# Interleaving three mixers, and letting the scheduler pick ScalarE or VectorE, in a two-layer hybrid decoder trunk

## The chip, the cores and the metric

The kernel runs on all 8 cores of one Trainium2 chip, two dies of four cores. Every core does the same program on its own prompt sequence of 2048 positions and 16 sample tokens; no core talks to another. The metric is the device time of the slowest core in microseconds (us). Most runs of one kernel agree within 0.3%. Some executions fall into a slower state, whatever the kernel: one die shows a lower granted clock and is over 1% longer.

The views of the profile use short names: PE is TensorE (PEld its weight loads), DVE is VectorE, ACT is ScalarE, POOL is GpSimd, SP is SyncE; L12 is line 12 of that run's kernel.py. PSUM is the memory that takes PE's results; this kernel uses it as eight banks.

## The reference, cut to what matters

```python
D_MODEL = 1024; SEQ = 2048; DEPTH = 2; C_A = C_B = 384; C_C = 256; K_A = 31; K_B = 3; CHUNK = 128; D_FF = 2816

def mixer(h, buf_a, buf_b, w_in, ...):
    z = h @ w_in                                             # ONE input projection, 2432 columns
    a_val, a_gate, b_x, b_b, b_c, c_u, c_v = jnp.split(z, SPLITS, axis=-1)
    hist_a = jnp.concatenate([buf_a, a_val * jax.nn.sigmoid(a_gate)], axis=1)             # A
    ya = jax.nn.silu(layernorm(causal_dwconv(hist_a, dw_a) + dw_a_bias, ln_a_g, ln_a_b))
    hist_b = jnp.concatenate([buf_b, b_c * b_x], axis=1)                                  # B
    yb = b_b * causal_dwconv(hist_b, conv_b_w)
    u = jax.nn.gelu(c_u)                                                                  # C
    vn = layernorm(jax.nn.gelu(c_v), ln_c_g, ln_c_b)
    yc = u * chunk_spatial(vn, w_s, b_s)
    return jnp.concatenate([ya, yb, yc], axis=-1) @ w_o, ...

for i in range(DEPTH):
    x = x + mixer(rmsnorm(x, norm_mix_g[i]), ...)
    gate, up = jnp.split(rmsnorm(x, norm_ffn_g[i]) @ w_ffn_in[i], 2, axis=-1)
    x = x + (jax.nn.silu(gate) * up) @ w_ffn_out[i]
return rmsnorm(x, norm_final_g)
```

## The kernel before

The kernel is written as a list of operations with their buffers. A list scheduler inside it (the "placer") then simulates the engines with rough costs and fixes, once and for all, the order in which each engine will execute. The order in the source sets an operation's priority (`due`); the placer departs from it when something later is ready earlier. ScalarE pays for a change of its function table, so an operation of another table set is put off by 3000 ns of priority. A matmul ahead of the program's order (`nd is not base`) gets a PSUM bank only while three of the eight are free.

```python
pick = None
for nd in cand[e]:
    if self._ready(nd, base, free) <= s + 30.0:
        d = nd.due
        if e == "act" and nd.table and nd.table != table:
            d += 3000.0
        if pick is None or d < pick[0]:
            pick = (d, nd)
# ... (cut)
def _ready(self, nd, base, free):
    # ... (cut)
    if new:
        if len(free) < new or (nd is not base and len(free) < 3):
            return 1e12
        r = max(r, min(free)[0])
```

The start: five column blocks (of 256, 272 and three times 512 columns, in this order) are loaded, normalised and projected for mixer A. Squares, Ln and Exp of the norms and the sigmoid of the gate are all ScalarE's.

```python
def sq_one(b, m):                        # 8 of these make one block's sum of squares
    act(AF.Square, sqt[si][:, 0:n], xT[:, m, c0:c0 + n], [b_x[m][b]], [b_sqt[si]])
    mm(pi[:, 0:n], [(ones_b[:], sqt[si][:, 0:n])], [b_sqt[si], b_const], pi, i == 0, i == 7)
# ... (cut)
def unit_a(b, j):
    pg = proj(("in", l, j), 0, b)                            # gate, one PSUM bank
    act(AF.Sigmoid, E[:, 0:n], pg[:, 0:n], [pg], [bE])       # another table set than Ln and Exp
    pv = proj(("in", l, j), 1, b)
    tt(phased(hist_a[:, j, :])[:, h0:h0 + nh], by(pv), by(E), ALU.mult, [pv, bE], [B[("ha", b)]])
```

The mixer's order, and the last step of mixer A. The convolution borrows the space of three of the eight residual rows (`xT[:, 5:8]`); `x_back` fetches them again.

```python
for q in range(2):
    for b in order:
        unit_cu(q, b)                    # all of u
# ... (cut)
for cp in range(8):
    unit_cv(cp)                          # v, its LayerNorm and the spatial product
    if cp >= 1:
        unit_conv(conv.popleft())        # mixer A's convolution, 12 of these
# ... (cut)
for j in range(3):
    for b in order:
        unit_b(j, b)                     # mixer B, three slices
        if conv:
            unit_conv(conv.popleft())
# ... (cut)
def ln_silu(g2):                         # mixer A's result, out to memory and back as yaC
    # ... (cut)
    k.dma("sp", yscr[l, j]..., poly[:, 8 * j:8 * j + 8, 4:4 + NN], ...)
    k.dma("sp", yaC[:, j, :], yscr[l, j], reads=[B[("yscr", j)]], writes=[B[("ya", j)]])

def x_back():
    # ... (cut)
    k.dma("sp", xT[:, 5:8, c0:c0 + n], src[:, :, c0:c0 + n], writes=[b_x[m][b] for m in range(5, 8)])
```

## Time and profile before

| before | |
|---|---|
| time, median of the first 4 runs | 1483.86 us (1482.32 to 1485.8) |
| PE, DVE, ACT busy | 95%, 40%, 26% |
| start and first mixer, until the first feed-forward flows | 286.6 us |
| first feed-forward, unbroken on PE | 466.8 us |
| second mixer | 237.0 us |
| second feed-forward, unbroken on PE | 466.2 us |
| end: last norm and output | 25.3 us |

The stages come from the chain of waits, which has one unbroken PE piece for each feed-forward; the 25.3 is a median over the cores. These are the two pieces in the kernel before (columns: start in us, length in us, what; x counts instructions), on its slowest core. The gap between the end of the first and the start of the second, 990.41 - 286.60 - 466.77, is the second mixer.

```profile
286.60 466.77 PE ps L482 x2683
...
990.41 466.21 PE ps L482 x2681
```

### The profile page before, as it was taken

The numbers are of one execution on the slowest core, as the hardware profiler recorded it, in microseconds if no ns is written. First come the engines' busy times: TensorE is split into PE (matmuls) and PEld (weight loads), VectorE is DVE, ScalarE is ACT, GpSimd is POOL, SyncE is SP. The second block draws the span as 40 slices with busy tenths as digits, with TensorE's granted clock in tenths as the row PEclk, the third lists the DMA queues.
The fourth block names the chain that finished last, engine by engine and source line by source line (L and its number), as shares of the span: only waits on it lengthen the run. The fifth ranks groups of instructions, "written<-read, shape, count | busy, mean of one in ns | idle before, by whom it ended". The sixth has DMA issues, their size and how long they took to land.

```text
span 1481.9 us, 23505 instructions; the slowest of 8 cores (1477.1 to 1481.9 us)
## 1 busy us (share of the span) xinstructions
PE 1405.1 (95%) x8288; PEld 798.4 (54%) x8288; DVE 594.3 (40%) x1179; ACT 385.9 (26%) x748; POOL 78.4 (5%) x156
## 2 busy tenths in 40 slices
PE   2797999999999999999999999999999999999995
PEld 1346654655555555555555755465555555555553
DVE  1536678632222222222282587863222222222237
ACT  3423633431110011111262452343111001111124
POOL 0002100000000000000000210000000000000000
PEclk9998999999999999999999999999999999999998
DMA  9744571124122221222243558021412312121106
GB/s 229 168 100 82 102 192 25 31 42 72 22 48 40 43 38 35 35 36 53 50 105 92 105 102 200 16 33 26 72 21 48 53 29 39 34 45 20 30 1 230
DMA packets 51490, 101.56 MB, mean 69 GB/s; under 512 B 5104, under 2 KB 25104, under 8 KB 51344
## 3 DMA queue, kind: packets, MB, share of 16 engines
q0 software_dynamic: 16704, 56.63, 22.9%
q1 hardware_dynamic: 34672, 43.43, 10.0%
q8 instruction: 70, 1.15, 0.3%
q14 instruction: 44, 0.36, 0.1%
HBM read 138.51 MB, written 19.63 MB: 107 GB/s over the span
## 4 chain that ended last, share of the span: by engine, by line
PE 88%; DVE 6%; issue 3%; DMA 1%; ACT 1%; POOL 0%; SPq 0%; DVEq 0%; ACTq 0%; POOLq 0%
PE ps L482 88%; DMA xT<-x_in 1%; DVE shr L470 1%; DVE hT L470 1%; ACT shr L460 1%; DVE bnst L818 1%; DVE xT L470 1%; DVE vtok L478 0%; DVE hT L467 0%; DVE xT L467 0%; ACT shr L464 0%; POOL rs L824 0%; DVE bnmv L820 0%; SPq L204 0%; DVE tC L470 0%
## 5 line engine op out<-in xcount | busy, mean ns | idle before, releaser
L482 PE MATMUL ps<-hT,ring 128*128 128x512 bf16 (+3 forms) x5168 | 924.3, 338 | 11.0 <-DVE hT L467 6.5
L482 PEld LDWEIGHTS ps<-hT,ring 128*128 128x128 bf16 x5168 | 505.4, 98 | 408.0 <-issue 18.6
L467 DVE TENSOR_TENSOR gT<-ps,fs 128x512 bf16<-128x512 f32 (+2 forms) x220 | 129.4, 588 | 478.4 <-PE ps L482 478.4
L482 PE MATMUL ps<-gT,ring 128*128 128x512 bf16 (+2 forms) x1760 | 311.8, 338 | 0.0
L460 ACT ACTIVATE fs<-ps 128x512 f32<-128x512 f32 (+2 forms) x220 | 113.1, 514 | 639.4 <-PE ps L482 603.9
L482 PEld LDWEIGHTS ps<-gT,ring 128*128 128x128 bf16 x1760 | 171.9, 98 | 135.3
L467 DVE TENSOR_TENSOR xT<-ps,xT 128x512 f32<-128x512 f32 (+2 forms) x240 | 139.3, 586 | 221.3 <-PE ps L482 221.1
L460 ACT ACTIVATE shr<-xT 128x512 bf16<-128x512 f32 (+2 forms) x224 | 114.6, 548 | 215.3 <-DVE xT L467 119.1
L470 DVE SCALAR_TENSOR_TENSOR hT<-xT,pD,shr 128x512 bf16<-128x512 f32 (+2 forms) x160 | 95.2, 642 | 40.9 <-ACT shr L460 40.9
L482 PE MATMUL ps<-shr,ones_b 128*128 128x512 bf16 (+2 forms) x200 | 53.7, 352 | 39.7 <-ACT shr L460 38.4
L467 DVE TENSOR_TENSOR hist<-ps,ev 128x512 bf16<-128x512 f32 (+1 forms) x60 | 34.8, 582 | 75.7 <-PE ps L482 61.1
L482 PE MATMUL ps<-yaC,ring 128*128 128x512 bf16 (+1 forms) x240 | 56.1, 339 | 0.0
L204 POOL DMA_DIRECT2D ring<-w_fi x44 | 23.2, 528 | 604.3 <-PE ps L482 604.3
L482 PEld LDWEIGHTS ps<-shr,ones_b 128*128 128x128 bf16 x200 | 19.6, 99 | 63.6 <-issue 50.8
L460 ACT ACT_TABLE_LOAD x27 | 34.6, 1283 | 28.5 <-PE ps L482 15.8
L482 PE MATMUL ps<-u_t,ring 128*128 128x512 bf16 (+2 forms) x160 | 41.4, 341 | 0.0
L470 DVE SCALAR_TENSOR_TENSOR shr<-hist,pAB,shr 128x512 f32<-128x512 bf16 (+1 forms) x60 | 36.8, 640 | 2.6 <-DVE shr L470 0.5
L204 POOL DMA_DIRECT2D ring<-w_fo x32 | 16.9, 530 | 318.2 <-PE ps L482 302.2
L482 PEld LDWEIGHTS ps<-yaC,ring 128*128 128x128 bf16 x240 | 23.6, 98 | 18.7 <-issue 0.8
L482 PE MATMUL ps<-poly,ring 128*128 128x256 bf16 x240 | 31.7, 288 | 1.8 <-ACT gv L460 1.2
L482 PE MATMUL ps<-ring,hT 128*128 128x256 bf16 (+1 forms) x272 | 31.0, 273 | 0.3 <-ACT gv L460 0.3
L467 DVE TENSOR_TENSOR xT<-xT,lnA 128x512 f32<-128x512 f32 x48 | 30.1, 684 | 0.1
(79 smaller groups left out, 434.7 us busy)
## 6 DMA issues: line engine op xcount, KB each, us to landing
ring<-w_fi POOLq DMA_DIRECT2D x44, 512.0 KB, 5.2
ring<-w_fo POOLq DMA_DIRECT2D x32, 352.0 KB, 4.3
ring<-w_in POOLq DMA_DIRECT2D x18, 512.0 KB, 7.3
ring<-w_tp POOLq DMA_DIRECT2D x12, 640.0 KB, 9.7
xT<-x_in SPq DMA_DIRECT2D x6, 1024.0 KB, 19.3
y_out<-xT SPq DMA_DIRECT2D x6, 1024.0 KB, 5.0
ring<-w_o POOLq DMA_DIRECT2D x8, 512.0 KB, 5.2
hscr<-hist SPq DMA_DIRECT2D x6, 512.0 KB, 11.1
```

The lines of the kernel that those rows point to most:

```text
L204: fn = lambda eng: eng.dma_start(out=out, in_=in_)
L460: k.op("act", lambda e: e.activation(out=ap(out), in_=ap(in_), func=func, bias=bias, scale=scale), reads, writes, width(out), SETS.get(func))
L467: k.op("dve", lambda e: e.tensor_tensor(out=ap(out), in0=ap(a), in1=ap(b), op=op), reads, writes, width(out))
L470: k.op("dve", lambda e: e.scalar_tensor_tensor(out=ap(out), in0=ap(in0), scalar=scalar, in1=ap(in1), op0=op0, op1=op1), reads, writes, wid ...
L482: k.node("pe", [((lambda e, p=p: e.matmul(ap(p[0]), lhsT=p[1], rhs=p[2], start=p[3], stop=p[4])), max(width(p[0]), 40) * 0.43, p[5] if len ...
L818: k.op("dve", lambda e, t=t: e.bn_stats(out=bn[0:np_, t, :], in_=G(t)), [bG], [B[("bn", z)]])
```

## The change

Its intent is to fill PE's bubbles in the mixers: interleave work that loads VectorE with projections that load PE, let elementwise work go to whichever of ScalarE and VectorE would finish it first, send mixer A's result ahead of the residual, and let PE run further ahead in PSUM. The diff, cut to its core:

```diff
+        def either(self, choices, reads, writes, n):        # a node with alternatives
...
-                if len(free) < new or (nd is not base and len(free) < 3):
+                if len(free) < new:
+                    return 1e12
+                if nd is not base and sum(1 for b in self.live if b.T > base.T) >= self.BANKS_AHEAD:   # 4
                     return 1e12
...
-            act(AF.Square, sqt[si][:, 0:n], xT[:, m, c0:c0 + n], [b_x[m][b]], [b_sqt[si]])
+            square(sqt[si][:, 0:n], xT[:, m, c0:c0 + n], [b_x[m][b]], [b_sqt[si]])   # ACT or DVE
...     (bias add and copies of the convolution, copy and first tap of mixer B: the same way)
-                    k.dma("sp", xT[:, 5:8, c0:c0 + n], src[:, :, c0:c0 + n], writes=[...])
+                    k.dma("sp", xT[:, 5:8, c0:c0 + n], src[:, :, c0:c0 + n],
+                          [B[("yscr", j)] for j in range(3)] + [B[("ya", j)] for j in range(3)], [...])
...     (weights: a dictionary, fetched in the order of first use, in place of a fixed list)
-            for q in range(2):
-                for b in order:
-                    unit_cu(q, b)
...     (the loops over unit_cv and unit_b of before)
+            for b in order:
+                unit_cu(0, b)
+                unit_cu(1, b)
+                for cp in range(8):
+                    if blk(2 * cp) == b:
+                        unit_cv(cp)
+                unit_b(0, b)
...
+                convs((0, 1, 1, 2, 2)[order.index(b)])
...
+            convs(6)
+            for j in (1, 2):
                 for b in order:
                     unit_b(j, b)
+                    convs(2 if j == 1 and b != order[4] else 0)
```

Because weights are now fetched on demand and mixer B's first slice ("in", 0, 5) has no entry in the list of held loads, it is fetched at the very start, in the middle of the input.

The whole diff also holds back the set-up of mixer C's mask until the last block is normalised.

## The prediction

> **What bounds the kernel now.** I read the cores first, to know whether a die was disturbed. It is not: the dies differ by 0.8 us in 1480, at one clock.
>
> ```profile
> die 0 (median of its cores): 1479.8 us, clock 0.989
> die 1 (median of its cores): 1479.0 us, clock 0.988
> ```
>
> Then the page: busy shares, the slices, and the chain that ended last.
>
> ```profile
> PE 1405.1 (95%) x8288; PEld 798.4 (54%) x8288; DVE 594.3 (40%) x1179; ACT 385.9 (26%) x748; POOL 78.4 (5%) x156
> ...
> PE   2797999999999999999999999999999999999995
> ...
> DVE  1536678632222222222282587863222222222237
> ...
> PE 88%; DVE 6%; issue 3%; DMA 1%; ACT 1%; POOL 0%; SPq 0%; DVEq 0%; ACTq 0%; POOLq 0%
> ```
>
> PE carries 88% of the chain. The two flat stretches of 9s are the feed-forward blocks, which no part of the change can shorten. What can move is where the PE row falls under 9 or the DVE row climbs to 6 to 8: the start, the two mixers, the end. PE 95% busy overstates its use, since ends of matmuls are modelled, so I counted columns. In full flow, in the last feed-forward, 11 matmuls of 512 columns take 2.54 us of which the last is 0.38, so one costs (2.54-0.38)/10 = 0.216 us, 0.422 ns a column. Times the columns of the matmuls listed in each stretch this gives useful PE time; the rest is lost time. Stretch by stretch (PE, PEld, DVE, ACT, POOL busy, then PE clock, DMA share, GB/s):
>
> ```profile
> 0.00:70.00 70.00, 34.12 (x149) 16.73 (x150) 24.39 (x48) 30.35 (x58) 3.49 (x10) 0.98 0.86 210
> 70.00:120.00 50.00, 50.00 (x306) 29.01 (x304) 15.58 (x37) 13.76 (x25) 1.78 (x4) 1.00 0.49 114
> 120.00:170.00 50.00, 39.20 (x346) 29.17 (x344) 38.37 (x109) 22.22 (x45) 12.20 (x24) 0.90 0.44 72
> ...
> 220.00:240.00 20.00, 16.53 (x96) 8.82 (x94) 19.59 (x46) 3.12 (x7) 0.53 (x1) 1.00 0.32 90
> ...
> 1440.00:1482.00 42.00, 26.31 (x156) 15.01 (x154) 28.57 (x52) 20.95 (x42) 0.00 (x0) 0.85 0.59 203
> ```
>
> Lost by columns: 46 us in 0 to 70; 13 in 120 to 170 (the chunk mixer C and the convolution of layer 0), 9.5 in the same phase of layer 1 (830 to 880); 3.5 in 220 to 240 and 5 in 920 to 950 (the gated mixer B), plus 1.5 each just before the two feed-forwards; 17 in the last 32 us. Together about 97 us. In 120 to 170 DVE is busy 38 of 50 us, yet in the 50 us before it only 16, while PE was full: the work is badly placed in time. In 220 to 240 DVE is saturated (19.6 of 20) and ACT nearly idle (3.1).
>
> What VectorE does there, and the DMA queue just before:
>
> ```profile
> L467 DVE TENSOR_TENSOR xT<-ps,pPP 128x512 f32<-128x512 f32 x24 | 15.7, 684 | 4.2 <-PE ps L482 3.9 <-issue 0.3
> L474 DVE TENSOR_SCALAR shr<-hist,pAB 128x512 f32<-128x512 bf16 x18 | 8.7, 481 | 0.6 <-ACT hist L464 0.6
> L460 ACT ACTIVATE shr<-xT 128x512 bf16<-128x512 f32 x144 | 84.4, 622 | 177.2 <-DVE xT L467 99.8 <-PE ps L482 75.2 <-DVE hT L470 2.0
> ```
>
> ```profile
> 198.76 0.80 SPq L204 DMA_DIRECT2D yscr<-poly  x1
> 199.65 8.47 SPq L204 DMA_DIRECT2D xT<-x_in  x5
> 208.28 6.57 SPq L204 DMA_DIRECT2D yaC<-yscr  x3
> ```
>
> The second fence matters: the return of the residual (five transfers, 3.1 MB) is queued ahead of the mixer A result that the output projection needs (yaC), so that result starts 9 us late.
>
> **What the Trainium skill says.** "VectorE: DVE Perf Modes", The TRN2 errata: an fp32 tensor_tensor takes (N+151)/0.96 ns, 691 for 512; the trace has 684 to 692. "ScalarE: Activation LUTs", What ACT_TABLE_LOAD costs: 186 ns + 0.833 a column, about 93 more per pointer operand, back-to-back ones overlapping by about 93. That is 613 for a square of 512 (trace 622), and 585 for 256 columns with two pointers (trace: 596). The same section has the table load at 1283 ns; the trace has 27 at a mean of 1283. "TensorE: Matmul & The Clock Gate", What's actually happening: PE drops to half rate after about 3.4 us idle. The trace agrees: after a wait of 4.46 us the clock of 130 to 140 is 0.56, so a bubble costs more than its own length. "DMA: Bandwidth & Descriptors", Queues, rings and completion order: each DMA engine takes turns among its queues; so an extra weight load shares bandwidth with the input.
>
> **The change part by part.**
> 1. *Order in the mixer.* Before: all of u, then eight v units with convolutions, then B. After: per block u, v, the first B slice and some convolutions. Matmuls are unchanged. A v unit costs DVE 2x(424+182+413+476+410) = 3.8 us, eight of them 30.5 us, packed against 14 us of projection. Spread over u, v, B0 and six convolutions (14+14+14+9 = 51 us of PE, with 30.5+3.4+4 = 38 us of DVE), PE becomes the slower one. I expect the lost 13 and 9.5 us to fall to 4 and 3.5: gain 15.
> 2. *Work that may go to either engine.* The 12 bias adds of a layer (684 ns of DVE each) can go to ACT as two activations, estimated from the skill's formula 2x493-93 = 0.9 us; squares and copies (ACT about 0.61) can go to DVE at 0.69; the 15 first taps of mixer B in a layer go to ACT, about 0.6 each. In the B phase DVE spends per 512-block 3x(481+748+748+684) = 8 us, 32 a layer, against 20.6 us of PE projection. Without the 481s it is 26, and ACT has room.
> 3. *yaC before the residual.* It no longer waits behind 8.5 us of queueing. Output projections of finished blocks can fill PE holes while DVE does B. The price: the last three row blocks of the residual arrive later, after five projections of the first block (5x1.7 us) at best. Parts 2 and 3 together: 3.5+5+1.5 of loss to about 4, gain 6.
> 4. *PSUM rule.* A matmul ahead of program order could take a bank only if three of eight were free; now up to four ahead-banks may be live, down to none free. It lets PE run ahead, and can also let ahead work sit on banks. No own gain credited.
> 5. *Weights on demand.* The slice of B0 now has a fresh ring place and no hold, so it is fetched right behind the first slice, in the input phase. On the software queue 3.28 MB took 29.6% of 70 us on all engines; so 0.52 MB costs an estimated 3.3 us, and block arrivals slip by about that.
> 6. *Start.* Blocks go round a loop of Ln and Exp 1.3, eight scalings on DVE 5.4 and a PE wait of 3 us, about 10 us each. Sharing squares with DVE, idle 5 us between blocks, may save 2 us on two blocks: 4 us. Four matmul groups of B0 can fill idle PE, but their second halves wait for the history buffer to be written out and keep banks. With part 5: gain 1, very unsure.
> 7. *End.* DVE is busy 28.6 of 42 us with residual adds and final scalings, which stay on DVE. Gain 0 to 1; taken as 0. Delaying the setup of masks: DVE work of 1.5 us moved only; 0.
>
> Sum: 15 + 6 + 1 = 22 us; 1484 - 22 = 1462; I shade it to **1460 us**, because bubbles that vanish also keep the PE clock up.
>
> **The rivals.**
> A. *The wait moves rather than vanishes.* Three weight slices (12 of the ring's 26 KB a partition) now stay live together through the interleaved phase. Taps for convolutions 4 and 5 can load only after the last u, later ones after the last v and B0, each taking 9.7 us to land. For: ring arithmetic. Against: B1's weights do not hang on those, so PE has 14 us of other work. If it bites in both layers: 5 to 8 us back, 1467 to 1470.
> B. *The start gets worse.* The extra load delays the second block, whose arrival (26.4 us) is on the chain, and held banks starve PE. For: DMA share 0.86 in 0 to 70, and that chain. Against: from 33 us the loop, not arrival, sets the pace. Time: 1465 to 1472.
> C. *Much more is won at the start:* more PE backlog done before 66 us, because ACT, freed from squares, serves the waiting sigmoids sooner. For: 46 us lost there, the largest pool. Against: table switches, and DVE has 5.4 of scaling plus 2 of gating per block. Time: 1440 to 1450.
> D. *Mixer losses are PE-only bubbles of latency, not DVE load:* then balancing gives little, 1475. DVE at 38 of 50 busy, and the idle 16 before, speak against it.
>
> **Range and chances.** A or B in part, or C in part, move the centre by 10 either way; two of them together by 15 to 18. Range 1442 to 1475. Two per cent below 1483.9 is 1454.2, 6 us under the centre, which needs C or a near-total recovery: 0.34. Within 2%: 0.63. Slower by over 2% would need a PSUM block of 30 us: 0.03.
>
> **What would show it.** Step 1: in the phase after the sigmoids DVE busy is spread at 7 to 8 tenths over some 60 us, with no PE wait on the v scalings (6.8 us before) and no clock under 0.9; ACT has bias activations. Steps 2 and 3: yaC is issued ahead of the residual, and the B phase has no PE wait on DVE over 1 us. Step 5: the third weight load within 5 us of the start, the last input block landing near 51 us. Feed-forward unchanged at 466 us of unbroken chain. I am wrong if the mixer stretches lose as much as before, or if the gain comes from the first 70 us.

## The result, and the profile after

The changed kernel takes 1450.2 us, the median of 8 runs (1448.9 to 1451.59). All runs of the kernel before have the median 1484.67. The ratio is 0.9769, with a 95% interval of 0.9759 to 0.9779. A ratio here is always the mean time of one kernel's fast runs over that of the other's of the same rounds, so not quite the ratio of the medians. Executions in which one die ran at a lower clock are left out of the means. The kernel is faster by 2.3%, some 34 us, where 24 were predicted.

The changed kernel's page, in the order of the lines that the prediction shows:

```profile
PE 1397.7 (96%) x8288; PEld 796.2 (55%) x8288; DVE 611.7 (42%) x1206; ACT 385.0 (27%) x731; POOL 78.8 (5%) x156
...
PE   3999999999999999999999999999999999999995
...
DVE  2657997522223222223573488762222332222237
...
PE 88%; DVE 4%; issue 2%; SPq 2%; DMA 2%; ACT 1%; DVEq 0%; POOL 0%; ACTq 0%; POOLq 0%
```

The second digit of the PE row went from 7 to 9: that is the start, from about 37 to 74 us. The fourth went from 7 to 9: that is the first mixer. VectorE as a whole is busy for 17 us more (611.7 against 594.3), so the gain is not relief of VectorE. It is work done at other moments. On the chain, SyncE's queue and the transfers have a larger share (0 to 2% and 1 to 2%), VectorE a smaller one (6 to 4%).

The same stretches as before, on the slowest core (us; PE, PEld, DVE, ACT, POOL busy; PE clock, DMA share, GB/s):

```profile
0.00:70.00 70.00, 42.16 (x229) 23.39 (x230) 30.11 (x66) 28.22 (x48) 3.50 (x10) 0.98 0.85 208
70.00:120.00 50.00, 50.00 (x325) 29.54 (x322) 29.28 (x70) 21.14 (x34) 6.96 (x14) 1.00 0.52 116
120.00:170.00 50.00, 47.96 (x369) 31.50 (x364) 41.36 (x100) 26.16 (x56) 8.29 (x17) 0.97 0.60 97
...
220.00:240.00 20.00, 20.00 (x94) 9.09 (x93) 14.24 (x23) 7.95 (x12) 0.00 (x0) 1.00 0.00 1
```

In 120 to 170 PE is busy for 48 us rather than 39, at a clock of 0.97 rather than 0.90. VectorE's work has moved into the 50 us before, 29 us where there were 16. And in the first 70 us PE issued 229 matmuls instead of 149.

The chain of waits of the kernel after (start, length, what):

```profile
34.04 18.29 DMA xT<-x_in
52.87 10.47 DMA ring<-w_in
63.48 1.91 PE ps L520 x12
...
66.87 72.22 PE ps L520 x478
...
262.51 466.41 PE ps L520 x2682
...
957.32 466.21 PE ps L520 x2681
```

At the start the chain of this core now goes through input and weight transfers until 63 us and then, but for two squares of 1.29 us, through PE for 72 us unbroken. On cores 0, 2, 3, 5 and 6 it goes through the third block's norm and scalings until 47 to 50 us and then through PE and the same two squares. The norms of the last two blocks, which it followed in the kernel before, are otherwise off it there. The stages on the slowest cores: start and first mixer 286.60 to 262.51, 24.1 us less; second mixer 237.04 to 228.40, 8.6 less; the rest, by difference, 0.5, of which 0.36 is in the first feed-forward.

To split the first of these I counted useful PE time as in the prediction (columns of the matmuls times 0.422 ns). On the slowest core of each kernel:

| done by | 70 us | 100 us | 140 us | 180 us |
|---|---|---|---|---|
| before | 22.4 | 52.3 | 81.1 | 117.6 |
| after | 34.3 | 64.3 | 103.7 | 138.5 |
| difference | 11.9 | 12.0 | 22.6 | 20.9 |

So by 70 us the changed kernel is 11.9 us of PE work ahead (8.6 on core 3, where before had 25.9). The slowest core of before was also the one with least done by 70 us; by the medians of all eight cores the lead is 9.5 us (25.2 and 34.7). Between 100 and 180 us it gains another 8.9 (10.3 by the medians), and the last 3.2 of the 24.1 come after 180 us, in mixer B and the output projection.

What happened at the start is a matter of ScalarE's order. ScalarE in the kernel before (start, length, then engine, line, operation, out<-in, count and, in brackets, idle time and its releaser): the last norm's Exp, the switch of the table, the first of the waiting sigmoids.

```profile
60.14 0.63 ACT L460 ACTIVATE shr<-shr 128x512 f32<-128x512 f32 x1
61.89 1.28 ACT L460 ACT_TABLE_LOAD   x1 [1.12 <-PE ps L482]
63.18 0.38 ACT L460 ACTIVATE ev<-ps 128x256 f32<-128x256 f32 x1
```

PE of the same kernel just then: it stops after 24 matmuls, and what lets it go on is that sigmoid.

```profile
59.04 3.64 PE L482 MATMUL ps<-hT,ring 128*128 128x512 bf16 x24
63.71 1.09 PE L482 MATMUL ps<-hT,ring 128*128 128x272 bf16 x8 [1.03 <-ACT ev L460]
```

ScalarE in the kernel after: the same table switch comes after the third norm, not the fifth, 18 us earlier.

```profile
41.42 0.63 ACT L486 ACTIVATE shr<-shr 128x512 f32<-128x512 f32 x1
...
44.15 1.28 ACT L486 ACT_TABLE_LOAD   x1
45.45 0.38 ACT L486 ACTIVATE ev<-ps 128x256 f32<-128x256 f32 x1
```

PE in the kernel after, while the fifth block was still coming in (until 52.3 us) and the fourth and fifth had their norms still ahead of them:

```profile
48.02 11.52 PE L520 MATMUL ps<-hT,ring 128*128 128x256 bf16 x64 [1.02 <-DVE hist L505]
```

In these twelve microseconds PE of before had small pieces, four matmuls of a norm or one of a projection, with waits for ScalarE and VectorE between them. That the order of ScalarE *causes* the gain is a theory at this point. The experiments test it.

The smaller signs that the prediction asked for. The elementwise work did spread: seven of the 24 bias adds went to ScalarE (14 activations of 256 columns, 472 ns each), and 16 of the 18 first taps of 512 columns. The groups view of the kernel after (line, engine, operation, shapes, count | busy us, mean ns | idle before and its releaser):

```profile
L789 ACT ACTIVATE xT<-ps,pPP 128x256 f32<-128x256 f32 x14 | 5.8, 472 | 4.0 <-PE ps L520 4.0
L954 ACT ACTIVATE shr<-hist,pAB 128x512 f32<-128x512 bf16 x16 | 10.5, 712 | 18.8 <-DVE hT L505 18.6
```

PE's waits on the v scalings fell from 6.8 us to 1.9 (the waits of PE in the kernel after: us in total, times, longest):

```profile
PE ps L520 <- DVE vtok L516: 1.9, 1, 1.9
```

And SyncE's queue sends yaC before the residual:

```profile
186.00 3.62 SPq L215 DMA_DIRECT2D yaC<-yscr  x3
197.49 4.07 SPq L215 DMA_DIRECT2D xT<-x_in  x5
```

### The profile page after: what moved, and what is told of

The parts are those of the page before. It is cut to its first block, busy times and chain, and to the rows that moved or that the text cites. A ratio compares the mean times of both kernels' runs of the same rounds, so it can differ in the third digit from the quotient of the medians.

```text
span 1448.7 us, 23408 instructions; the slowest of 8 cores (1445.8 to 1448.7 us)
## 1 busy us (share of the span) xinstructions
PE 1397.7 (96%) x8288; PEld 796.2 (55%) x8288; DVE 611.7 (42%) x1206; ACT 385.0 (27%) x731; POOL 78.8 (5%) x156
## 4 chain that ended last, share of the span: by engine, by line
PE 88%; DVE 4%; issue 2%; SPq 2%; DMA 2%; ACT 1%; DVEq 0%; POOL 0%; ACTq 0%; POOLq 0%
PE ps L520 88%; SPq L215 2%; DMA xT<-x_in 1%; DVE shr L508 1%; DMA ring<-w_in 1%; DVE xT L501 1%; DVE xT L508 1%; DVE hT L505 0%; ACT shr L493 0%; ACT shr L486 0%; DVE hist L505 0%; DVE xT L505 0%; DVE hT L508 0%; DVE shr L494 0%; ACT shr L497 0%
## 5 line engine op out<-in xcount | busy, mean ns | idle before, releaser
L493 ACT ACTIVATE shr<-xT 128x512 bf16<-128x512 f32 (+2 forms) x175 | 92.3, 547 | 208.9 <-DVE xT L505 101.9
L505 DVE TENSOR_TENSOR hist<-ps,ev 128x512 bf16<-128x512 f32 (+1 forms) x60 | 34.8, 582 | 45.5 <-PE ps L520 35.3
L494 DVE TENSOR_TENSOR shr<-xT 128x512 bf16<-128x512 f32 (+2 forms) x49 | 29.0, 611 | 20.9 <-DMA xT<-x_in 17.1
L520 PE MATMUL ps<-ring,hT 128*128 128x256 bf16 (+1 forms) x272 | 31.5, 273 | 0.5 <-DMA ring<-w_in 0.5
L501 DVE TENSOR_TENSOR xT<-xT,lnA 128x512 f32<-128x512 f32 x48 | 30.2, 684 | 0.0
```

The costliest lines, as they stand in the source:

```text
L493: k.either({"act": lambda e: e.activation(out=out, in_=a, func=AF.Square), "dve": lambda e: e.tensor_tensor(out=out, in0=a, in1=a, op=ALU. ...
L494: "dve": lambda e: e.tensor_tensor(out=out, in0=a, in1=a, op=ALU.mult)}, reads, writes, width(out))
L501: f = lambda e: e.tensor_tensor(out=out, in0=a, in1=b, op=op)
L505: k.op("dve", lambda e: e.tensor_tensor(out=ap(out), in0=ap(a), in1=ap(b), op=op), reads, writes, width(out))
L520: k.node("pe", [((lambda e, p=p: e.matmul(ap(p[0]), lhsT=p[1], rhs=p[2], start=p[3], stop=p[4])), max(width(p[0]), 40) * 0.43, p[5] if len ...
```

## The experiments

Twelve kernels ran, each beside runs of the kernel before on its own chip. All gave correct results. For each I give two stages besides the time: *first* is the time to the first feed-forward, *second* the second mixer, each a median over the cores whose chain shows it. *First* is counted back from the end of the first feed-forward by the 466.4 us that it takes in the kernel after, since in some runs (s1, x4) its unbroken piece begins 2 us late. The kernel before has 284.3 and 237.0, the one after 261.0 and 228.3; feed-forwards and end never moved by more than 0.6 us. Two theories of the start stood against each other. S: the earlier sigmoids make the gain. Q: the freedom of the squares, which shortens each norm, makes it. The expectations name a third, P: the new PSUM rule makes it; m4 and x4 bear on that. For the mixers, the question was which part of the change made which gain, and whether the parts add up or act only together (I, interaction).

### s1: before, with the sigmoids of two blocks ahead of the fourth norm

```diff
-            act(AF.Square, sqt[si][:, 0:n], xT[:, m, c0:c0 + n], [b_x[m][b]], [b_sqt[si]])
+            act(AF.Square, sqt[si][:, 0:n], xT[:, m, c0:c0 + n], [b_x[m][b]] + list(after), [b_sqt[si]])
...
-                        sq_one(b, m)
+                        sq_one(b, m, [B[("ha", order[0])], B[("ha", order[1])]] if i == 3 and m >= 4 else ())
```

> The kernel before, with one dependency added: the last four squares of the fourth input block wait until the gating of the first two blocks is done, so ScalarE takes the waiting sigmoids before the last two norms. Theory S (the start is gained because the sigmoids are served before the last two norms, which lets TensorE work off the first blocks while the rest of the input arrives): about 10 us faster than before, 1472 to 1477. Theory Q (the start is gained because squares are shared with VectorE) and theory P (because of the new PSUM rule): no gain, 1482 to 1488, or slower by the two extra table loads.

Measured 1475.22 us (1474.71 to 1476.96), ratio 0.9941 [0.9925, 0.9956]. First 271.1, 13.2 less than before; second 242.3, 5.3 more. ScalarE's timeline shows the switch at 50.6 us instead of 61.9:

```profile
50.57 1.28 ACT L460 ACT_TABLE_LOAD   x1 [6.62 <-PE ps L482]
51.87 0.38 ACT L460 ACTIVATE ev<-ps 128x256 f32<-128x256 f32 x1
```

One added dependency, with all other parts of the old kernel as they were, is worth 13 us before the first feed-forward, although it makes ScalarE load tables 39 times, not 27. About half of it is there by 70 us (32.0 us of PE work by the median of the cores, 6.8 more than before). Theory S stands: Q is not needed for it. Where the 5.3 went is in the waits of PE (us in total, times, longest):

```profile
PE ps L482 <- DMA yaC<-yscr: 8.7, 1, 8.7
```

Now PE reached the output projection before mixer A's result was there. I come back to this wait at m3.

### s2: after, with mixer B's first slice held until the last input block is in

```diff
-                     ("in", 0, 4): [b_x[7][2]], ("tp", 0, 0): [b_x[7][2]]}
+                     ("in", 0, 4): [b_x[7][2]], ("tp", 0, 0): [b_x[7][2]], ("in", 0, 5): [b_x[7][2]]}
```

> The changed kernel, with the sixth weight slice (first slice of mixer B) held until the last input block has landed, as the fifth is. The placer then puts the sigmoids after four norms, not after three. Theory S: a large part of the gain at the start is lost, 1454 to 1460. Theories Q and P: nothing lost, and the input lands some 4 us earlier, 1446 to 1450.

Measured 1456.99 us, ratio 0.9815 [0.98, 0.9831]; first 267.3, second 228.2. The number is in the range of S, and ScalarE did switch after the fourth norm, not the third (51.97 us on the slowest core). But the test is not clean. VectorE's timeline has an operation of the sample tokens that waits for a small load, and it stands on the chain:

```profile
100.30 0.66 DVE L505 TENSOR_TENSOR hs<-hs,pAB 128x480 f32<-128x480 f32 x1 [7.84 <-DMA hs<-sa_t]
```

This wait explains a part of the 6 us at most. PE stood for VectorE by 3.7 us between 60 and 115 us on this core, 1.3 on core 1:

```profile
PE ps L520 <- DVE hist L505: 3.7, 1, 3.7
```

And about half of the loss was there before it: by 70 us the cores' median of PE work is 31.3 us, against 34.7 in the kernel after. The cores tell more. Cores 1 and 7 switched tables at 47.1 us and ended the first stage at 262.2 and 262.3; cores 0 and 6 switched at 54.3 and 54.0 and ended it at 269.8 and 269.4, with the same wait of VectorE (5.6 and 5.6 us against 5.4 and 5.5). That fits S, but on cores 0 and 6 the input was late too (the Ln of the second block's norm came at 34.1 and 33.1 us, against 26.9 and 26.1). So the run leans towards S and does not settle it.

### s3: after, with the norms' squares fixed on ScalarE

```diff
-            square(sqt[si][:, 0:n], xT[:, m, c0:c0 + n], [b_x[m][b]], [b_sqt[si]])
+            act(AF.Square, sqt[si][:, 0:n], xT[:, m, c0:c0 + n], [b_x[m][b]], [b_sqt[si]])
```

> The changed kernel, with all squares of the norms on ScalarE again; its order of sigmoids and norms on ScalarE stays that of the changed kernel. Theory S: within 3 us of the changed kernel, 1448 to 1454. Theory Q: most of the gain at the start lost, 1458 to 1462.

Fast runs 1454.51 to 1456.5 us (one slow, 1731), ratio 0.9805 [0.9787, 0.9822], between the two expectations. First 265.6, 4.6 more than after. The table switch still comes early (44.86 us). So Q holds a part: the squares on VectorE are worth 4.6 us there. It is a contribution beside S, not in its place.

### s4: after, with the slice held and the sigmoids forced early as in s1

```diff
-                     ("in", 0, 4): [b_x[7][2]], ("tp", 0, 0): [b_x[7][2]]}
+                     ("in", 0, 4): [b_x[7][2]], ("tp", 0, 0): [b_x[7][2]], ("in", 0, 5): [b_x[7][2]]}
...
-                        sq_one(b, m)
+                        sq_one(b, m, [B[("ha", order[0])], B[("ha", order[1])]] if i == 3 and m >= 4 else ())
```

> The changed kernel with the sixth slice held and the sigmoids forced ahead of the last two norms by the dependency of the first run. Theory S: the gain is back without the early load that delays the input, 1444 to 1450. Under Q or P no different from the second run.

Measured 1449.52 us (1448.7 to 1449.91), ratio 0.9764 [0.9747, 0.9781]; first 259.8, second 228.3. It equals the changed kernel: the intervals overlap almost wholly. So the early fetch of the slice is not what the start gain hangs on; with the slice held and the sigmoids forced early, the whole gain is there. It is the fastest kernel, but not one that can be told from the changed kernel.

### m1: after, with the old order in the mixers

```diff
-            for b in order:
-                unit_cu(0, b)
-                unit_cu(1, b)
...     (the interleaved loops of the change)
+            for q in range(2):
+                for b in order:
+                    unit_cu(q, b)
...     (all of v, then mixer B, as before; everything else stays)
```

> The changed kernel with the mixer's old order of units (all u, then v with convolutions, then mixer B). If the order is the main cause of the gain in the mixers (step 1, 15 us), the second layer's mixer (228.3 us from the end of one feed-forward to the start of the next in the changed kernel, 237.0 before) goes back to 233 to 238, and the time to 1462 to 1475, the first layer losing as much and something at the start besides, because the slice of mixer B is then fetched late. If the free choice of engine is the cause, the second mixer stays at 228 to 231.

Two fast runs, 1461.58 and 1464.38 (two were slow, 1510 and 1635), ratio 0.9841 [0.9806, 0.9877]. First 267.1, second 233.3: 6.1 and 5.0 back, as expected in size. The order is worth 11 us of the 34. Part of the 6.1 is the start again: in the old order ScalarE switches to the sigmoids only at 51.41 us, and PE has done 31.5 us of work by 70 us, 2.8 less than after.

### m2: after, with the engines of the mixers' elementwise work fixed

```diff
-                          "act": [lambda e, i=i: e.activation(out=V[:, i, :], ..., func=AF.Identity, bias=...) for i in range(2)]},
...
-                copy2(vbf[i3][:], V, [bV], [B[("vb", i3)]])
-                square(vsq[i3][:], V, [bV], [B[("vs", i3)]])
+                acopy(vbf[i3][:], V, [bV], [B[("vb", i3)]])
+                act(AF.Square, vsq[i3][:], V, [bV], [B[("vs", i3)]])
...     (the copy and the first tap of mixer B: fixed as in before)
```

> The changed kernel with the mixers' work put back on its old engines (bias adds and first taps on VectorE, copies and squares of the convolution on ScalarE); the norms' squares stay free. If VectorE's load in the mixers counts (step 2, about 3 to 4 us of the 6 for steps 2 and 3), 1452 to 1457, and the second mixer 230 to 232. If the order alone already makes TensorE the bound, 1449 to 1452.

Fast runs 1458.4 to 1460.04 us (one slow, 1498), ratio 0.9816 [0.9782, 0.985]. First 264.9, second 231.6: 3.9 and 3.3 back. The freedom of engines in the mixers is worth 7 us, a little more than I had expected.

### m3: after, with the residual no longer held behind yaC

```diff
-                    k.dma("sp", xT[:, 5:8, c0:c0 + n], src[:, :, c0:c0 + n], [B[("yscr", j)] ...] + [B[("ya", j)] ...],
+                    k.dma("sp", xT[:, 5:8, c0:c0 + n], src[:, :, c0:c0 + n], (),
```

> The changed kernel without the wait of the residual's return for mixer A's result. If the late result was a cause of the loss in the mixer B phase (step 3), 1452 to 1456, with TensorE waiting at the start of the output projection in both layers. If not, 1449 to 1451.

A miss, and the most instructive run. Fast runs 1475.31 and 1476.31 (two slow ones left out), ratio 0.9928 [0.9894, 0.9961]: undoing one dependency loses some 24 of the 34 us. First 272.7, second 239.6, 11.7 and 11.3 more. SyncE's queue issues the five residual transfers first, which takes it 11.6 us, and only then yaC:

```profile
180.42 2.53 SPq L215 DMA_DIRECT2D yscr<-poly  x3
183.10 11.56 SPq L215 DMA_DIRECT2D xT<-x_in  x5
194.82 3.67 SPq L215 DMA_DIRECT2D yaC<-yscr  x3
```

PE's timeline shows the price, and the second mixer has the same wait once more, with 12.8 us:

```profile
214.38 1.44 PE L520 MATMUL ps<-hT,ring 128*128 128x512 bf16 x3 [9.99 <-DMA yaC<-yscr]
```

The transfers of yaC took 15.0 us from issue to landing (median) against 9.0 in the changed kernel, so they are both issued late and slowed down.

### m4: after, with the old PSUM rule

```diff
-                if len(free) < new:
-                    return 1e12
-                if nd is not base and sum(1 for b in self.live if b.T > base.T) >= self.BANKS_AHEAD:
+                if len(free) < new or (nd is not base and len(free) < 3):
                     return 1e12
```

> The changed kernel with the old PSUM rule (three of eight banks free before a matmul may run ahead). I credited the new rule with nothing: 1448 to 1452. If running ahead on fewer free banks is what fills the holes, 1455 to 1465.

Fast runs 1456.46 and 1456.79 (two slow), ratio 0.9799 [0.9766, 0.9832]. First 268.3, second 227.9. The rule, which I had credited with nothing, is worth 7.3 us before the first feed-forward and nothing in the second mixer. Useful PE time by 70 us, on the slowest core, is 31.0, 3.3 below after, so a bit under half of it is lost by 70 us and the rest after that.

### x1: before, with the residual held behind yaC

```diff
-                    k.dma("sp", xT[:, 5:8, c0:c0 + n], src[:, :, c0:c0 + n], writes=[...])
+                    k.dma("sp", xT[:, 5:8, c0:c0 + n], src[:, :, c0:c0 + n],
+                          [B[("yscr", j)] for j in range(3)] + [B[("ya", j)] for j in range(3)], [...])
```

> The kernel before, with only the residual's return held back until mixer A's result is back in SBUF. In the changed kernel this hold is worth 25 us, because without it TensorE waits 10.0 and 12.8 us for that result. In the kernel before, TensorE waited for VectorE there, never for that result. Theory I (interaction: the hold pays only once the mixers are fast enough to need the result early): 1479 to 1486, second mixer 235 to 238. Theory H (the hold was worth its 6 to 12 us a layer by itself): 1462 to 1473.

Measured 1481.55 us, beside 1487.56 for the kernel before on that chip; ratio 0.9968 [0.9946, 0.999]. First 283.9, second 235.5: 0.4 and 1.5 less. The same dependency whose removal cost 23 us in the changed kernel gives about 2 in the old one, about 5 by the ratio. Theory I holds for this part. No wait for yaC stands among PE's waits there. In both source orders two slices of mixer B follow the convolution; what differs is how soon PE is through with them. From PE's last convolution matmul to its first product of the output projection the kernel before takes 59.7 and 60.7 us in the two layers, which covers the late yaC, the kernel after 55.8 and 53.2. That this is the whole reason is not shown: in s1 the wait of 8.7 us came in the second layer only.

### x2: before, with the new order, weights on demand and the residual held

The edit is that of x1, the interleaved loops of the change, and its weight ring. The engines stay fixed and the PSUM rule is the old one.

```diff
-            for q in range(2):
-                for b in order:
-                    unit_cu(q, b)
...
+            for b in order:
+                unit_cu(0, b)
+                unit_cu(1, b)
...
-        while key not in self.at:
-            name, size, src = self.items[self.next]
+        if key not in self.at:
+            size, src = self.items[key]
```

> The kernel before with the new mixer order, the weights fetched on demand and the residual held; engines and the PSUM rule stay old. ScalarE then serves the sigmoids early, as in the changed kernel. If the single reversals add up (engines 7, squares 5, PSUM rule 7 us on top of 1450), 1466 to 1472. If they share losses, 1456 to 1463. If order, early sigmoids and hold are not the main part, above 1475.

Fast runs 1469.59 and 1471.84 (three slow), ratio 0.9892 [0.9863, 0.9921]. First 277.4, second 231.3. From here to the changed kernel 16.4 us of the first stage are missing. The reversals of the other three parts were 3.9 (m2), 4.6 (s3) and 7.3 (m4), together 15.8. In the second mixer 3.0 are missing, and the reversals were 3.3 (m2), -0.7 (s3) and -0.4 (m4), together 2.2. From this side, then, the parts add up. By 70 us x2, with its table switch at 46.83 us, had done 30.2 us of PE work on its slowest core, 7.8 more than before, and that core's first stage is 8.0 shorter; by the medians of the cores the two figures are 5.2 and 6.9. So without the engines and the PSUM rule, the new order gained at most some 2 us in the first mixer itself, and 5.7 in the second.

### x3: after, with a sigmoid group forced ahead of each of the last three norms

```diff
-                        sq_one(b, m)
+                        sq_one(b, m, {2: [B[("ha", order[0])]], 3: [B[("ha", order[1])]], 4: [B[("ha", order[2])]]}.get(i, []) if m >= 4 else ())
```

The slice is held as in s2.

> The changed kernel, sixth slice held, and each block's gating forced ahead of the norm two blocks later, so that the sigmoids of the first block come before the third norm. If TensorE's holes before 45 us are of the same cause (banks held by waiting sigmoids), 1443 to 1448. If by then it is the arrival of the input that limits, or the extra table loads cost as much, 1448 to 1456.

A miss: 1458.74 us, ratio 0.9814 [0.9795, 0.9833], some 7 us over the changed kernel. First 271.2. By 70 us only 24.9 us of PE work were done on the slowest core. Of PE's waits until 270 us, these two were below 1 us in the kernel after:

```profile
PE ps L520 <- DMA ring<-w_in: 9.1, 2, 4.6
PE ps L520 <- DVE shr L494: 5.6, 1, 5.6
```

So earlier is not better without end. Each block's norm now waits for another block's gating, and the held weights of the later slices arrive after PE wants them. The cores differ widely, though: cores 3 and 4, whose input came some 3 us sooner, had done 32.9 and 34.8 us by 70 us and ended the first stage at 264.3 and 263.4. So a part of the loss goes with a late input, and the run does not part the two.

### x4: before, with the new PSUM rule

```diff
-                if len(free) < new or (nd is not base and len(free) < 3):
+                if len(free) < new:
+                    return 1e12
+                if nd is not base and sum(1 for b in self.live if b.T > base.T) >= self.BANKS_AHEAD:
                     return 1e12
```

> The kernel before with only the new PSUM rule. Taking the rule out of the changed kernel cost 7 us, all of it in the first layer, none in the second. If the rule works at the start by itself (the placer then puts sigmoids ahead of the last norm), the time from the start to the first feed-forward falls by 4 to 10 us and the second mixer stays at 236 to 238: 1475 to 1481. If it pays only together with the new order, 1482 to 1487.

Measured 1475.43 us, beside 1487.64 for the kernel before on that chip; ratio 0.9924 [0.9896, 0.9952]. First 272.2, 12.1 less; second 242.2, 5.2 more. The table switch moved to 53.39 us, ahead of the last norm. So the rule does at the start what s1 did by hand: the placer can let PE go on, which changes what ScalarE finds ready first. The total came out as expected; the second mixer did not. ScalarE's timeline has the switch after the fourth norm:

```profile
53.39 1.28 ACT L466 ACT_TABLE_LOAD   x1
```

In the second mixer no wait for yaC is there this time. PE's waits sum to 12.6 us against 9.8 in the kernel before, spread over seven causes, the largest 4.4; the rest of the 5.2 us I did not settle. Any edit changes the placer's greedy choices in both layers, so a stage can move by some 5 us without a reason of its own, and differences of that size in single experiments should be read with that in mind.

Read together, the timelines say which part of the change moved the switch. It comes after the fifth norm in the kernel before and in x1; after the fourth in x4, m1 and s2, which have the new PSUM rule but not both the new order and the early slice; and after the third where both of these are there, even without the new PSUM rule (x2, m4).

## Why the prediction was right or wrong

The time fell inside the range (1442 to 1475), 10 us below the centre, and with a ratio of 0.9769 beyond the 2% line: the outcome that had been given 0.34, not the likelier 0.63. By stages the account is this:

| stage | predicted gain | measured |
|---|---|---|
| start, first 70 us | 1 | 11.9 |
| first mixer, C and convolution | 9 (13 to 4) | 8.9 (between 100 and 180 us) |
| first layer, mixer B to output projection | 3 (half of 6) | 3.2 |
| second mixer | 9 (9.5 to 3.5, and the other 3) | 8.6 |
| feed-forwards, end | 0 | 0.5 by difference |

(By the medians of the eight cores the first two rows are 9.5 and 10.3.)

The start is the term of the sum that was mis-sized. It is step 6, "gain 1, very unsure", which had also been told as rival C. I treated the start as a loop over blocks of about 10 us, in which only the length of a norm counts (squares, 4 us, less the weight load). I had seen that the sigmoids wait, and priced that only as a rival with "table switches" against it. In fact ScalarE's order decided most of it. One dependency that moves the sigmoids forward gave 13.2 us before the first feed-forward in the old kernel (s1; 6.8 of them by 70 us, against 9.5 for the whole change), and in the new one it kept the whole gain without the early slice (s4). By its own sign ("wrong if the gain comes from the first 70 us") about a third of the gain speaks against the prediction. A switch to sigmoids and back costs two loads of 1.28 us; what it frees is PE's work on the finished blocks (two in s1, three in the kernel after) ahead of the norms of the last two.

Step 1, the order in the mixers: the mechanism was right. VectorE's work is spread (16 to 29 us in 70 to 120), waits on the v scalings fell from 6.8 to 1.9 us, the clock in 120 to 170 is 0.97. The reversal gives 11 us (m1) where the step said 15, and x2 shows that in the first layer the order needed the other parts for it. The lost times that the sum starts from were a little low: counted again by the same rule they are 47.6 us in 0 to 70 (46 was said), 14.2 in 120 to 170 (13) and 10.2 in 830 to 880 (9.5); in the kernel after, 120 to 170 loses 5.0.

Steps 2 and 3: 7 us for the engines (m2), where both together had been given 6. The hold of the residual is an enabling part: about 2 us by stages alone (x1), 23 when it is taken out of the complete change (m3). The prediction saw its mechanism, the queue, but took yaC's 9 us of delay as a matter of filling holes (and its sum takes the 1.5 us before a feed-forward once, where two were named). It is a wait that the new order would have exposed.

Step 4, "no own gain credited", was wrong: 7.3 us (m4), alone 12.1 before the first feed-forward (x4; 6.6 of them by 70 us). That the mixer terms come out nearly exact in the table is thus partly luck: the order gave less than step 1 said, the PSUM rule and the engines more.

Step 5, the early slice: two weight loads are issued together within 3 us of the start (the sign had named the third load and 5 us; the third comes at 8.72), and the last input block landed at 52.3 us where the sign had said near 51. The third held load, which waits for the fourth block, was issued at 44.17 instead of 40.25, and the one that waits for the last block at 52.87 instead of 48.03: 3.9 and 4.8 us of slip (3.4 and 4.0 by the medians of the eight cores), where 3.3 had been estimated. The step was right and a little small, and it did not set the time.

Step 7 was right: nothing at the end (25.3 to 25.2 by the median of the cores).

Of the rivals, A did not bite; no PE wait on tap weights stands in the changed kernel. B's cause came true (the slip) without its effect. C is what happened. D falls: balancing did pay.

## What to carry to other kernels

When a list scheduler orders an engine with modes, look for work of the other mode that waits while that engine finishes a series: a switch in the middle can be far cheaper than the idle time of the engine behind it. When you move work so that a consumer comes sooner, check what was hidden behind the moved work, above all transfers queued behind bulk ones; such a dependency can be worth little alone and much of the gain together. And measure a compound change by taking parts out as well as putting them in alone, for the two answers can differ five- to tenfold (x1 and m3).

## What the Trainium skill lacked or had wrong

- "ScalarE: Activation LUTs", Table sets: the hidden batching unit, gives the rule to batch activation calls by set, and about 2.7 us for a switch. Here the order that batched the norms at the start was the slower one: s1, with 39 table loads instead of 27, starts its first feed-forward 13.2 us earlier. And a switch cost 1.28 us alone: in the kernel after the load starts at 44.15 and the next activation at 45.45. x3 shows that the reverse can be overdone.
- "TensorE: Matmul & The Clock Gate", Seeing it yourself, says that a die goes to 13/16 of its clock once three of its cores run dense matmuls. Here all eight cores do, and the changed kernel's runs show 0.990 to 0.995 on every core. Only some executions show a lower clock, in every one with its cores on record on one die alone: in s3's slow run of 1731 us one die had 0.812 to 0.826, the other 0.991 to 0.993; in other slow runs a die had values between, such as 0.947 to 0.969 in one of m1.
- No page that I read sizes what a result that is wanted soon (here yaC, 1.5 MB) loses behind bulk transfers (3.1 MB) in the same issuing queue. Here SyncE needed 11.56 us to issue five residual transfers in m3 (4.07 in the kernel after, when they came last), yaC landed in 15.0 us rather than 9.0, and PE stood for 10.0 and 12.8 us.
- No page that I read says that ScalarE's order sets how far PE can run ahead. Here a projection stood still until a sigmoid of another table set (PE released by it at 63.71 us), and relaxing the rule for PSUM banks moved that table switch from 61.89 to 53.39 us (x4).
